# Gathering tokens for two experts at a time instead of four in a one-core decoder layer

## The chip, the cores and the metric

The kernel runs on one core of a Trainium2 chip. A core has TensorE (PE; its weight loads are listed as PEld), VectorE (DVE), ScalarE (ACT), GpSimd (POOL) and SyncE (SP, which here only issues DMAs), and 16 DMA engines. The metric is the device time of one execution in microseconds; the median of three executions of the kernel before is 1170.96 us (1170.91 to 1171.41).

## The reference

One layer of a decoder for 256 tokens of width 2048: a mixing part (pooling, sparse attention, cross attention, gates) that updates `x`, and then a mixture of 16 experts. Only the experts are touched here:

```python
lg = h @ w_router_group                      # 4 groups
g_top = argmax(lg)                           # every token goes to one group
le_sel = (h @ w_router_expert) of that group # 4 experts in it
pe_top, e_local = lax.top_k(softmax(le_sel), 2)
combine = one_hot(e_id) * weights            # two experts of one group per token
a = einsum('bsd,edf->bsef', h, w_e_gate)     # 16 x 2048 x 512
b = einsum('bsd,edf->bsef', h, w_e_up)
act = silu(a) * b * combine
x = x + einsum('bsef,efd->bsd', act, w_e_down)
```

All of it is in float32. Gate, up and down weights of the 16 experts are 192 MB.

## The kernel before, in words

The mixing part runs first (to about 720 us of the span), and loads of expert weights are mixed into its end. The experts follow in eight *pairs* of two experts (`pair`, L1101). A pair uses 24 weight tiles of 1 MB: 8 for gate, 8 for up, 8 for down (in the first pair gate and up alternate, table `FIRST`). Each weight tile of gate or up holds two k-tiles (128 rows of the 2048) for both experts, and takes 4 matmuls of 512 columns; each down tile takes 8 matmuls of 256 columns. The trace lists each of these float32 matmuls as two records.

*Gathering.* The tokens of four experts (a *quad*, one group) are picked at once by `Gather`. A 0/1 matrix `sel` (256 tokens by 4 x 64 places) is built on DVE from `slot`; the normalised input goes to 64 places per expert by matmuls: for each k-tile, `x2` is split into a high and a low part `xs` (ACT copies, DVE subtracts; three buffers, `split`), and four matmuls (high and low, two token halves) with `xs` as weights and `sel` as moving data give the gathered columns in PSUM. DVE multiplies them by the gain into `xg`, 16 k-tiles by 256 columns. One `step` does two k-tiles: 8 matmuls of 256 columns. The first quad is gathered between the gate and up tiles of pair 0; the later ones in pairs 1, 3 and 5: one step before and one behind the turning of the activations, and one behind each of six down tiles. Pairs 0, 2, 4 and 6 also compute the row factors of the quad (`factors`, four matmuls `sm<-cw,sel`) and turn `sel` for the way back (`back`, four transposes `sm<-ident,sel`, evacuated to `selT`).

*Scattering.* Behind each 512 columns of the down product, `scatter` splits them into high and low (`ob`), multiplies by `selT` (4 matmuls `sm<-ob,selT`) and adds the result into `x2`. A token belongs to one group, so the scattering of one quad never touches the tokens of the next; a quad's own tokens are gathered before its scattering.

*Order.* In this part each of PE, DVE, ACT and the loads on SP is pinned to the order in which the code is written. Weight tiles go round a ring of buffers (`order`: 4 `hq`, 9 `ex`, 8 of `raw` and `mx`: 21); one tile more, number 15 of the first pair, has its own buffer until pair 0 ends (`we15`). SP issues loads in the order of use, and each waits until PE has finished with the buffer's last tile. All PE work of the experts has line L840 (transposes L845), all DVE and ACT work L129.

Of the kernel before, what the change touches and what calls it, by code (L numbers as in the profile page):

```python
# [20 lines left out]
P = 128  # L21
NT = 2
# [33 lines left out]
def layer_kernel(tc, x, xT, memT, pos, cst, band, gains, bgate, wmem, wxq, widx, wkqvp, wpg, wgb, wo, wr, we, out):  # L56
# [5 lines left out]
    def pool(name, bufs=1, side=None, space=None, reuse="tile"):  # L62
        kw = {}
        if space is not None:
            kw["space"] = space
        else:
            kw["side"] = side or "left"
            kw["reuse_waits"] = reuse
        cm = tc.tile_pool(name=name, bufs=bufs, **kw)
        return cm, cm.__enter__()  # L70
# [67 lines left out]
    def sm_tile(shape, name="sm"):  # L138
        return sm.tile(shape, F32, tag="sm", name=name)
# [66 lines left out]
    def load(dst, src):  # L206
        tc.keep_in_program_order(nc.sync.dma_start(dst, src))
# [549 lines left out]
    def prefetch():  # L757
        pr, i = todo.popleft()
        kind = order.popleft()
        if kind == "raw":  # L760
            w = raw.tile([P, 4, 512], F32, tag="raw", name="wr")
        elif kind == "hq":
            w = htp.tile([P, 4, 512], F32, tag="hq", name="wh")
        elif kind == "ex":
            w = pools["exp"][1].tile([P, 4, 512], F32, tag="ew", name="we")
        else:
            w = mgp.tile([P, 4, 512], F32, tag=kind, name="wm", bufs=2)
        order.append(kind)
        if (pr, i) == (NE // 2 - 1, 23):
            load(w[:, 0:2], we[pr, i, :, 0:2])  # L770
            load(w[:, 2:4], we[pr, i, :, 2:4])
        else:
            load(w, we[pr, i])
        ahead.append(w)
# [63 lines left out]
    def pe(*a, **k):  # L838

        i = mm(*a, **k)  # L840
        tc.keep_in_program_order(i)
        return i

    def turn(ps, src):
        tc.keep_in_program_order(nc.tensor.transpose(ps, src, ident))  # L845
# [72 lines left out]

    c_w, wk = pool("work", side="right")

    pools["x"] = pool("early", side="right")
    et = pools["x"][1].tile([P, 4, 512], F32, name="we15")
    load(et, we[late])
    ahead.insert(use.index(late), et)

    def rt(shape, name):
# [11 lines left out]


    C = [P, NT * 5, 4, 4]  # L940
    xg0 = wk.tile([P, KD, 256], F32, tag="xg", name="xg")
    w = xg0[:, 14:16].rearrange("p a b -> p (a b)")
    Rc = w[:, 0:40].rearrange("p (t e) -> p t e", e=4)
    rank = w[:, 40:80].rearrange("p (t g e) -> p t g e", t=NT, e=4)
    ohg = w[:, 490:498].rearrange("p (t g) -> p t g", t=NT)
    c1 = w[:, 80:240].rearrange("p (t i j) -> p t i j", i=4, j=4)
    c2 = w[:, 240:400].rearrange("p (t i j) -> p t i j", i=4, j=4)
    E = w[:, 400:440].rearrange("p (t g e) -> p t g e", t=NT, e=4)
    EQ = 4
    SQ = EQ * 64  # L950

    def part(k, x0=None, dve=False):
# [36 lines left out]
    class Gather:  # L989
# [41 lines left out]

        def back(self, wp):

            self.selT = wp.tile([P, 2, S], F32R, tag="selT", name="selT")
            ps = sm_tile([P, 2, NT, P])
            for h in range(2):
                for t in range(NT):
                    turn(ps[:, h, t], self.flat[:, t, h * P : (h + 1) * P].bitcast(F32))
            A.activation(self.selT, ps.rearrange("p h t q -> p h (t q)"), AF.Copy)

        def factors(self):

            ps = sm_tile([P, 2, 2, 18])
            for h in range(2):
                for t in range(NT):
                    pe(ps[:, h], self.flat[:, t, h * P : (h + 1) * P], cw[:, t], start=t == 0, stop=t == NT - 1)
            self.f = wk.tile([P, 2, 2], F32, tag="fac", name="fac", bufs=2)
            fs = wk.tile([P, 2, 18], F32, tag="facs", name="facs")
            V.tensor_copy(fs, ps[:, :, 1])
            V.tensor_add(fs, fs, ps[:, :, 0])  # L1050
            for h in range(2):
                V.tensor_copy(self.f[:, h, 0:1], fs[:, h, NE : NE + 1])
                for e in range(2):
                    c = EQ * self.q + 2 * h + e
                    V.tensor_copy(self.f[64 * e : 64 * e + 64, h, 1:2], fs[64 * e : 64 * e + 64, h, c : c + 1])

    gf = cs[:, C_GFFN : C_GFFN + KD]
    ga = Gather(0, slot, parts0, xg0)
# [40 lines left out]
            next(open_.popleft(), None)  # L1099

    def pair(pr, slot_, store, ga):  # L1101
        hf = pr % 2

        def use_tile(ac, i):
            w = wtile()
            for kk in range(2):
                k = 2 * i + kk
                for e in range(2):
                    s0 = hf * P + 64 * e
                    pe(ac[64 * e : 64 * e + 64], ga.xg[:, k, s0 : s0 + 64], w[:, 2 * kk + e],  # L1110
                       start=k == 0, stop=k == KD - 1)

        def gathered(n):
            while 8 - len(ga.todo) < min(8, n):
                ga.step()

        nx = ga
        ag, au = acc_tile("gu"), None
        if pr == 0:
            au = acc_tile("gu")  # L1120
            for up, i in FIRST:
                gathered(i + 2)
                if (up, i) == (0, 7):
                    ga.factors()
                use_tile(au if up else ag, i)
                if (up, i) == (1, 0) and "x" in pools:
                    weights()
                    inorder.clear()
            if "x" in pools:
                close(pools.pop("x")[0])  # L1130
                pools["w2"] = pool("work2", side="right")
        else:
            for i in range(8):
                gathered(8)
                use_tile(ag, i)
                finish()
            if hf == 0:
                ga.factors()
            elif not store:
                nx = Gather(pr // 2 + 1, slot_, x0=ga.x0)  # L1140
                nx.split(3)
        w2 = pools["w2"][1]
        r2s, c1s = ga.f[:, hf, 0:1], ga.f[:, hf, 1:2]
        sg = w2.tile([P, FF], F32, tag="sg", name="sgm")
        A.activation(sg, ag, AF.Sigmoid, scale=r2s)
        V.scalar_tensor_tensor(sg, ag, r2s, sg, op0=ALU.mult, op1=ALU.mult)
        if au is None:
            au = acc_tile("gu")
            for i in range(8):
                use_tile(au, i)  # L1150
        for c in range(2):
            c = slice(c * FF // 2, (c + 1) * FF // 2)
            V.scalar_tensor_tensor(sg[:, c], sg[:, c], c1s, au[:, c], op0=ALU.mult, op1=ALU.mult)
        if hf == 0:
            ga.back(w2)
        elif nx is not ga:
            nx.step()
        aT = w2.tile([P, 4, P], F32, tag="aT", name="aT")
        for c in range(2):
            ps = sm_tile([P, 2, P])  # L1160
            for f in range(2):
                turn(ps[:, f], sg[:, (2 * c + f) * P : (2 * c + f + 1) * P])
            A.activation(aT[:, 2 * c : 2 * c + 2], ps, AF.Copy)
        if nx is not ga:
            nx.step()

        def scatter(ad, c0, n):
            ob = w2.tile([P, 2, 512], F32R, tag="ob", name="ob")[:, :, :n]
            A.activation(ob[:, 0], ad, AF.Copy)
            V.tensor_sub(ob[:, 1], ad, ob[:, 0])  # L1170
            yield
            for t in range(NT):
                ps = sm_tile([P, 512])[:, :n]
                for u in range(2):
                    pe(ps, ga.selT[:, hf, t * P : (t + 1) * P], ob[:, u], start=u == 0, stop=u == 1)


                ys = x2[:, t, c0 : c0 + n]
                V.tensor_add(ys, ys, ps)
                if store:  # L1180
                    nc.scalar.dma_start(out[t * P : (t + 1) * P, c0 : c0 + n], ys)

        def emit(ad, c0, n):

            g = scatter(ad, c0, n)
            next(g)
            open_.append(g)

        for n in range(4):
            ad = acc_tile("dn")  # L1190
            for i in range(2):
                if store and n == 3 and i == 1:
                    ad = acc_tile("dn")
                w = wtile()
                for k in range(4):
                    for e in range(2):
                        pe(ad[64 * e : 64 * e + 64, 256 * i : 256 * i + 256], aT[:, k, 64 * e : 64 * e + 64],
                           w[:, k, 256 * e : 256 * e + 256], start=k == 0, stop=k == 3)
                finish()
                if nx is not ga:  # L1200
                    nx.step()
                if store and n == 3:
                    emit(ad[:, 256 * i : 256 * i + 256], n * 512 + 256 * i, 256)
            if not (store and n == 3):
                emit(ad, n * 512, 512)
        if store:
            finish()
        return nx
# [34 lines left out]
            ga = pair(pr, slot, pr == NE // 2 - 1, ga)  # L1243

    close(pools["w2"][0])
    close(c_w)
    close(c_ht)
    close(c_ed)
# [86 lines left out]
```

## Time and profile before

| | |
|---|---|
| median of 3 runs | 1170.96 us |
| profiled execution | 1171.39 us, span 1169.4 us |
| PE busy | 1141.6 us, 98% |
| DVE busy | 579.1 us, 50% |
| ACT busy | 423.8 us, 36% |
| DMA | 342.44 MB, mean 293 GB/s |
| granted TensorE clock | 0.995 of full |

Busy time of PE is modelled, since matmuls are pipelined. So the distance from the start of one group of matmuls to the start of the next is the better measure of what it takes, and it is used below. A number in brackets behind a row of the timeline is idle time ahead of it, with what ended it.

### The profile page before, as it was taken

How to read it: one execution, taken by the hardware profiler on the slowest of the kernel's cores; microseconds unless marked ns; L12 is line 12 of the kernel's file. 1: busy time of each engine (PE TensorE's matmuls, PEld its weight loads, DVE VectorE, ACT ScalarE, POOL GpSimd, SP SyncE). 2: the span in 40 equal slices, each digit the busy share in tenths (PEclk: the TensorE clock that was granted, in tenths of full speed). 3: DMA queues.
4: the chain of work that ended last, by engine and by line, in shares of the span. 5: the costliest groups of instructions: out<-in, count | busy, mean ns of one | idle time of the engine just before them, and what ended most of it. 6: DMA issues, size and time to landing. Idle time of an engine off the chain costs nothing.

```text
span 1169.4 us, 14739 instructions
## 1 busy us (share of the span) xinstructions
PE 1141.6 (98%) x5847; PEld 786.6 (67%) x5847; DVE 579.1 (50%) x962; ACT 423.8 (36%) x672; POOL 28.9 (2%) x33
## 2 busy tenths in 40 slices
PE   8999999999999999999999999999999999999985
PEld 5788887888878888888888787454544645363423
DVE  7877468956636556556556445331412422250202
ACT  6665565445644444444444443211101201020000
POOL 3200000000000000000000000000000000000000
PEclk9999999999999999999999999999999999999998
DMA  9546554555545565565599859999999999999995
GB/s 384 188 149 225 180 180 153 180 180 174 208 174 203 192 212 199 191 208 203 190 340 363 316 192 351 423 423 426 426 427 426 427 426 427 427 425 427 426 428 216
DMA packets 50189, 342.44 MB, mean 293 GB/s; under 512 B 5696, under 2 KB 6336, under 8 KB 10432
## 3 DMA queue, kind: packets, MB, share of 16 engines
q1 hardware_dynamic: 46800, 331.93, 73.0%
q0 software_dynamic: 1728, 7.15, 1.7%
q10 hardware_dynamic: 1584, 2.34, 0.6%
q8 instruction: 48, 0.79, 0.2%
q14 instruction: 29, 0.24, 0.1%
HBM read 337.20 MB, written 4.19 MB: 292 GB/s over the span
## 4 chain that ended last, share of the span: by engine, by line


## 5 line engine op out<-in xcount | busy, mean ns | idle before, releaser
L282 PE MATMUL acc<-wh,hT 128*128 128x512 f32 (+1 forms) x1280 | 396.1, 388 | 0.0
L133 DVE TENSOR_TENSOR wl<-rawt,wh 128x1024 fp32r<-128x1024 f32 (+1 forms) x240 | 289.9, 1211 | 208.7 <-ACT wh L132 207.8
L132 ACT ACTIVATE wh<-rawt 128x1024 fp32r<-128x1024 f32 (+1 forms) x240 | 250.9, 1048 | 296.8 <-PE acc L282 289.9
L282 PEld LDWEIGHTS acc<-wh,hT 128*128 128x128 f32 x1280 | 238.3, 188 | 46.6 <-issue 0.3
L282 PE MATMUL acc<-wl,hT 128*128 128x512 f32 (+1 forms) x640 | 249.1, 389 | 0.0
L282 PEld LDWEIGHTS acc<-wl,hT 128*128 128x128 f32 x640 | 120.2, 188 | 23.9 <-DVE isc L593 0.3
L840 PE MATMUL gu<-we,xg 128*64 128x512 f32 x464 | 104.7, 596 | 4.6 <-DMA we<-in_we_dram 4.6
L282 PE MATMUL acc<-wh,mgT 128*128 128x512 f32 x256 | 80.3, 392 | 0.0
L840 PEld LDWEIGHTS gu<-we,xg 128*64 128x64 f32 x464 | 31.8, 137 | 68.9 <-issue 53.5
L129 DVE TENSOR_TENSOR x<-x,sm 128x512 f32<-128x512 f32 (+1 forms) x66 | 41.3, 668 | 32.6 <-PE sm L840 32.6
L129 ACT ACTIVATE ob<-dn 128x512 fp32r<-128x512 f32 (+1 forms) x33 | 19.2, 581 | 104.8 <-PE dn L840 98.2
L129 ACT ACTIVATE xs<-x 128x256 fp32r<-128x256 f32 x57 | 23.0, 415 | 90.0 <-PE sm L840 88.8
L282 PEld LDWEIGHTS acc<-wh,mgT 128*128 128x128 f32 x256 | 47.8, 188 | 10.0 <-issue 0.4
L129 DVE SCALAR_TENSOR_TENSOR sgm<-sgm,fac,gu 128x256 f32<-128x256 f32 x16 | 7.0, 478 | 92.0 <-PE gu L840 92.0
L282 PE MATMUL acc<-wl,mgT 128*128 128x512 f32 x128 | 50.5, 394 | 0.0
L129 DVE TENSOR_TENSOR ob<-dn,ob 128x512 fp32r<-128x512 f32 (+1 forms) x33 | 22.2, 673 | 55.9 <-ACT ob L129 55.9
L129 ACT ACTIVATE sgm<-gu,fac 128x512 f32<-128x512 f32 x8 | 5.5, 687 | 115.0 <-PE gu L840 68.0
L840 PE MATMUL gu<-wh,xg 128*64 128x512 f32 x200 | 45.1, 596 | 1.1 <-DMA wh<-in_we_dram 1.1
L840 PE MATMUL dn<-we,aT 128*64 128x256 f32 x384 | 45.6, 384 | 0.3
L840 PE MATMUL gu<-wm,xg 128*64 128x512 f32 x184 | 43.5, 593 | 0.5 <-DMA wm<-in_we_dram 0.5
L282 PE MATMUL acc<-wh,memT 128*128 128x512 f32 x128 | 41.8, 404 | 1.2 <-ACT wh L132 1.2
L840 PE MATMUL gu<-wr,xg 128*64 128x512 f32 x176 | 41.8, 595 | 0.5 <-DMA wr<-in_we_dram 0.5
(341 smaller groups left out, 1192.5 us busy)
## 6 DMA issues: line engine op xcount, KB each, us to landing
we<-in_we_dram SPq DMA_DIRECT2D x82, 1024.0 KB, 19.5
rawt<-in_wgb_dram SPq DMA_DIRECT2D x64, 1024.0 KB, 4.8
wh<-in_we_dram SPq DMA_DIRECT2D x37, 1024.0 KB, 19.6
wr<-in_we_dram SPq DMA_DIRECT2D x36, 1024.0 KB, 19.5
wm<-in_we_dram SPq DMA_DIRECT2D x36, 1024.0 KB, 19.5
rawt<-in_wkqvp_dram SPq DMA_DIRECT2D x24, 1024.0 KB, 4.8
rawt<-in_wo_dram SPq DMA_DIRECT2D x16, 1024.0 KB, 6.2
rawt<-in_wmem_dram SPq DMA_DIRECT2D x7, 1024.0 KB, 8.2
```

What stands on the lines that cost most here:

```text
L129: return lambda *a, **k: tc.keep_in_program_order(getattr(self.e, name)(*a, **k))
L132: pin(A.activation(hi, ps, AF.Copy))
L133: pin(V.tensor_sub(lo, ps, hi))
L282: m = mm(o, a[:, c], w[:, kk], start=st, stop=sp)
L840: i = mm(*a, **k)
```

## The change

`EQ`, the number of experts in one gather, goes from 4 to 2. `Gather` is made for each pair instead of each second pair; `sel` has 128 columns, `selT` half its rows, `xg` is 16 k-tiles by 128 columns, 8 KB per partition instead of 16 KB. The freed 8 KB hold one weight tile more, kind `e2`, which joins the ring (22 buffers) and is first loaded right behind `we15`.

Since two pairs now share a group's tokens, the next pair's tokens have to be gathered before the present pair's scattering changes them. `follow` turns `sel`, makes the next `Gather` and splits three parts; it stands ahead of the up tiles (in pair 0 behind gate and up). One step runs behind each of up tiles 1 to 7, writing the k-tiles of the same `xg` that the up matmuls have finished with, and the eighth behind the turning of the activations. In pair 0 all eight run among the first three down tiles. `finish`, which runs the waiting scatter, comes behind the steps instead of ahead of them.

```diff
+        elif kind == "e2":
+            w = pools["e2"][1].tile([P, 4, 512], F32, tag="e2", name="wn")
...
+    pools["e2"] = pool("more", side="right")
+    order.appendleft("e2")
...
     load(et, we[late])
+    prefetch()
...
-    xg0 = wk.tile([P, KD, 256], F32, tag="xg", name="xg")
+    xg0 = wk.tile([P, KD, P], F32, tag="xg", name="xg")
-    EQ = 4
+    EQ = 2
...
+        def follow():
+
+            ga.back(w2)
+            if store:
+                return ga
+            g = Gather(pr + 1, slot_, xg=ga.xg, x0=ga.x0)
+            g.split(3)
+            return g
...
             au = acc_tile("gu")
+            nx = follow()
             for i in range(8):
                 use_tile(au, i)
+
+                if i > 0 and nx is not ga:
+                    nx.step()
...
-        if hf == 0:
-            ga.back(w2)
-        elif nx is not ga:
-            nx.step()
+        if pr == 0:
+            nx = follow()
...
+                if nx is not ga:
+                    for _ in range(8 if n else 2 if pr == 0 else 1):
+                        nx.step()
                 finish()
-                if nx is not ga:
-                    nx.step()
```

On PE, pair 1 from its last up tiles on, in the kernel before (`sm<-sel,xs` x8 is one step of a gather, `gu` gate or up, `dn` down, `sm<-ident,sgm` the turning of the activations, `sm<-ob,selT` a scatter):

```order
L840 MATMUL gu<-wm,xg 64x512 x4
L840 MATMUL gu<-wr,xg 64x512 x4
L840 MATMUL sm<-sel,xs 128x256 x8
L845 MATMUL sm<-ident,sgm 128x128 x4
L840 MATMUL sm<-sel,xs 128x256 x8
L840 MATMUL dn<-wm,aT 64x256 x8
L840 MATMUL sm<-sel,xs 128x256 x8
L840 MATMUL dn<-wr,aT 64x256 x8
```

The same place in the changed kernel, from the end of the gate tiles on:

```order
L842 MATMUL sm<-cw,sel 128x36 x2
L847 MATMUL sm<-ident,sel 128x128 x2
L842 MATMUL gu<-we,xg 64x512 x8
L842 MATMUL sm<-sel,xs 128x128 x8
L842 MATMUL gu<-we,xg 64x512 x4
...
L842 MATMUL gu<-wm,xg 64x512 x4
L842 MATMUL sm<-sel,xs 128x128 x8
L847 MATMUL sm<-ident,sgm 128x128 x4
L842 MATMUL sm<-sel,xs 128x128 x8
L842 MATMUL dn<-wr,aT 64x256 x8
```

A step still has 8 matmuls, with 128 columns in place of 256. Every pair but the last now holds eight of them, where before only pairs 0, 1, 3 and 5 did.

On PE in pair 0, from the turning of the activations on, in the changed kernel (before, no step stands there):

```order
L847 MATMUL sm<-ident,sgm 128x128 x4
L842 MATMUL sm<-sel,xs 128x128 x8
L842 MATMUL dn<-wr,aT 64x256 x8
L842 MATMUL sm<-sel,xs 128x128 x16
L842 MATMUL dn<-wm,aT 64x256 x8
L842 MATMUL sm<-sel,xs 128x128 x16
L842 MATMUL dn<-wr,aT 64x256 x8
L842 MATMUL sm<-sel,xs 128x128 x24
L842 MATMUL sm<-ob,selT 128x512 x4
```

Four of the eight steps follow another step directly there, and the first scatter comes behind all of them.

On DVE in pair 1, from the multiplication by the gate on, in the changed kernel (`xg<-sm,cs` ends a step, `sgm<-sgm,fac,gu` is the product that the turning waits for):

```order
L129 SCALAR_TENSOR_TENSOR sgm<-gu,fac,sgm 128x512
L129 TENSOR_TENSOR sel<-cs,slot 128x128 x2
L129 TENSOR_TENSOR xs<-x_4893,xs 128x256 x4
L129 TENSOR_TENSOR xg<-sm,cs 128x256
...
L129 TENSOR_TENSOR xs<-x_4893,xs 128x256 x2
L129 TENSOR_TENSOR xg<-sm,cs 128x256
L129 SCALAR_TENSOR_TENSOR sgm<-sgm,fac,gu 128x256 x2
L129 TENSOR_TENSOR xg<-sm,cs 128x256
```

The product now stands behind the multiplication that ends the seventh step; before, it stood ahead of the first.

## Rows read from the trace of the kernel before

**Rows 1.** The page's 40 slices of the span: PE busy and DMA, in tenths.

```profile
PE   8999999999999999999999999999999999999985
...
DMA  9546554555545565565599859999999999999995
```

**Rows 2.** Busy time by windows, pairs 0 to 7: PE, PEld, DVE, ACT, POOL, clock, DMA share, GB/s.

```profile
725.64:781.36 55.72, 55.60 (x331) 26.89 (x330) 21.79 (x67) 9.70 (x22) 0.00 (x0) 1.00 1.01 420
781.36:837.54 56.18, 56.18 (x342) 28.97 (x342) 21.51 (x46) 9.66 (x23) 0.00 (x0) 1.00 1.01 426
837.54:886.47 48.93, 48.80 (x287) 21.89 (x284) 10.63 (x23) 4.29 (x8) 0.00 (x0) 1.00 1.01 427
886.47:942.61 56.14, 56.14 (x342) 28.92 (x340) 20.81 (x41) 9.69 (x23) 0.00 (x0) 1.00 1.01 426
942.61:991.53 48.92, 48.78 (x286) 21.88 (x284) 10.63 (x23) 4.29 (x8) 0.00 (x0) 1.00 1.01 427
991.53:1047.67 56.14, 56.14 (x342) 28.93 (x340) 20.81 (x41) 9.68 (x23) 0.00 (x0) 1.00 1.01 426
1047.67:1096.60 48.93, 48.80 (x286) 21.89 (x284) 10.63 (x23) 4.29 (x8) 0.00 (x0) 1.00 1.01 426
1096.60:1156.03 59.43, 51.09 (x278) 19.95 (x274) 9.59 (x16) 4.23 (x8) 0.00 (x0) 1.00 0.97 405
```

**Rows 3.** Timeline of PE in pair 7: start, us, engine, line, tiles, count, idle before.

```profile
1099.55 3.65 PE L840 MATMUL gu<-wh,xg 128*64 128x512 f32 x16
1103.78 1.94 PE L840 MATMUL gu<-wh,xg 128*64 128x512 f32 x8 [0.58 <-DMA wh<-in_we_dram]
...
1133.08 1.94 PE L840 MATMUL gu<-wm,xg 128*64 128x512 f32 x8 [0.52 <-DMA wm<-in_we_dram]
```

**Rows 4.** Timeline of PE, end of pair 2's up tiles and the turning.

```profile
863.57 1.89 PE L840 MATMUL gu<-wr,xg 128*64 128x512 f32 x8
865.29 1.89 PE L840 MATMUL gu<-wm,xg 128*64 128x512 f32 x8
867.11 0.66 PE L845 MATMUL sm<-ident,sel 128*128 128x128 f32 x4
867.76 0.83 PE L845 MATMUL sm<-ident,sgm 128*128 128x128 f32 x4
```

**Rows 5.** Timeline of PE, the first steps of quad 0 between gate and up tiles.

```profile
722.34 1.14 PE L309 MATMUL warm<-ident 128*128 128x128 f32 x8
723.32 2.33 PE L840 MATMUL sm<-sel,xs 128*128 128x256 f32 x16
725.64 3.65 PE L840 MATMUL gu<-wh,xg 128*64 128x512 f32 x16
729.23 1.22 PE L840 MATMUL sm<-sel,xs 128*128 128x256 f32 x8
730.38 3.65 PE L840 MATMUL gu<-wh,xg 128*64 128x512 f32 x16
```

**Rows 6.** Timeline of PE, the narrow matmuls of the factors in pair 4.

```profile
957.74 0.62 PE L840 MATMUL sm<-cw,sel 128*128 128x36 f32 x4
958.29 1.94 PE L840 MATMUL gu<-wr,xg 128*64 128x512 f32 x8
```

**Rows 7.** Groups by line and form from 690 us on: busy, mean ns, idle before.

```profile
L129 DVE TENSOR_TENSOR xs<-x,xs 128x256 fp32r<-128x256 f32 x57 | 23.5, 421 | 27.3 <-ACT xs L129 26.7
...
L129 ACT ACTIVATE xs<-x 128x256 fp32r<-128x256 f32 x57 | 23.0, 415 | 90.0 <-PE sm L840 88.8
...
L129 DVE TENSOR_TENSOR x<-x,sm 128x256 f32<-128x256 f32 x4 | 1.5, 418 | 1.0 <-PE sm L840 1.0
```

**Rows 8.** Busy time by windows of 2 us about the first extra load.

```profile
720.00:722.00 2.00, 1.88 (x17) 1.68 (x16) 1.83 (x9) 1.64 (x4) 0.00 (x0) 1.00 0.95 295
722.00:724.00 2.00, 1.74 (x16) 1.76 (x17) 1.15 (x5) 0.00 (x0) 0.00 (x0) 1.00 0.92 369
...
730.00:732.00 2.00, 2.00 (x12) 0.87 (x12) 1.25 (x9) 1.36 (x3) 0.00 (x0) 1.00 0.84 332
```

More of the change, by code (lines that the diff above doesn't have):

```diff
@@ L940, in layer_kernel @@
     C = [P, NT * 5, 4, 4]
-    xg0 = wk.tile([P, KD, 256], F32, tag="xg", name="xg")
-    w = xg0[:, 14:16].rearrange("p a b -> p (a b)")
+    xg0 = wk.tile([P, KD, P], F32, tag="xg", name="xg")
+    w = xg0[:, 12:16].rearrange("p a b -> p (a b)")
     Rc = w[:, 0:40].rearrange("p (t e) -> p t e", e=4)
@@ L1032, in back @@
         def back(self, wp):
[L1034 to L1039, printed above, removed]
-        def factors(self):
[L1043 to L1055, printed above, removed]
+            self.selT = wp.tile([P, S], F32R, tag="selT", name="selT")
+            ps = sm_tile([P, NT, P])
+            for t in range(NT):
+                turn(ps[:, t], self.flat[:, t].bitcast(F32))
+            A.activation(self.selT, ps.rearrange("p t q -> p (t q)"), AF.Copy)
+        def factors(self):
+            ps = sm_tile([P, 2, 18])
+            for t in range(NT):
+                pe(ps, self.flat[:, t], cw[:, t], start=t == 0, stop=t == NT - 1)
+            self.f = wk.tile([P, 2], F32, tag="fac", name="fac", bufs=2)
+            fs = wk.tile([P, 50], F32, tag="facs", name="facs")[:, :18]
+            V.tensor_copy(fs, ps[:, 1])
+            V.tensor_add(fs, fs, ps[:, 0])
+            V.tensor_copy(self.f[:, 0:1], fs[:, NE : NE + 1])
+            for e in range(2):
+                c = EQ * self.q + e
+                V.tensor_copy(self.f[64 * e : 64 * e + 64, 1:2], fs[64 * e : 64 * e + 64, c : c + 1])
     gf = cs[:, C_GFFN : C_GFFN + KD]
@@ L1101, in pair @@
     def pair(pr, slot_, store, ga):
-        hf = pr % 2
         def use_tile(ac, i):
@@ L1108, in use_tile @@
                 for e in range(2):
-                    s0 = hf * P + 64 * e
+                    s0 = 64 * e
                     pe(ac[64 * e : 64 * e + 64], ga.xg[:, k, s0 : s0 + 64], w[:, 2 * kk + e],
@@ L1136, in pair @@
                 finish()
-            if hf == 0:
[L1138 to L1141, printed above, removed]
-        w2 = pools["w2"][1]
-        r2s, c1s = ga.f[:, hf, 0:1], ga.f[:, hf, 1:2]
+            ga.factors()
+        w2 = pools["w2"][1]
+        r2s, c1s = ga.f[:, 0:1], ga.f[:, 1:2]
+        def follow():
[5 more added lines that the diff above has]
+            return g
         sg = w2.tile([P, FF], F32, tag="sg", name="sgm")
@@ L1153, in pair @@
             V.scalar_tensor_tensor(sg[:, c], sg[:, c], c1s, au[:, c], op0=ALU.mult, op1=ALU.mult)
-        if hf == 0:
-            ga.back(w2)
-        elif nx is not ga:
-            nx.step()
+        if pr == 0:
+            nx = follow()
         aT = w2.tile([P, 4, P], F32, tag="aT", name="aT")
@@ L1174, in scatter @@
                 for u in range(2):
-                    pe(ps, ga.selT[:, hf, t * P : (t + 1) * P], ob[:, u], start=u == 0, stop=u == 1)
+                    pe(ps, ga.selT[:, t * P : (t + 1) * P], ob[:, u], start=u == 0, stop=u == 1)
                 ys = x2[:, t, c0 : c0 + n]
@@ L1245, in layer_kernel @@
     close(pools["w2"][0])
+    close(pools["e2"][0])
     close(c_w)
```

## The prediction

> **What bounds the kernel now.** I read the 40 slices of the page first. PE is at nine tenths nearly throughout, and from about slice 25 on, where the experts are computed, the DMA is too [rows 1]. Two resources look full, and only one of them can set the pace at a time, so the second view is a table of windows cut at the pairs [rows 2]. The DMA moves 420 to 427 GB/s in pairs 0 to 6, whatever the pair holds. But the pairs do not last equally long: those with a gather of the next quad take 56.18, 56.14 and 56.14 us, those without 48.93, 48.92 and 48.93. Every pair uses 24 tiles, so a DMA that set the pace would make them equal. It is PE that does.
>
> What a pair would take at the DMA's pace is read in the third view, the timeline of the last pair. From 1103.78 on, each tile's first matmul waits for its load [rows 3]; from there to 1133.08 are 12 tiles, 29.30 us, or 2.44 us a tile and 58.6 us for 24. So PE begins with a stock of loaded tiles, eats them faster than they come (48.9 or 56.1 us against 58.6), and runs out of them only in pair 7. There it waits. Pair 7 has no factors and no turned `sel` of its own, so PE's work in it is that of pair 6 less 0.55 us for the four factor matmuls [rows 6] and 0.65 us for the four transposes [rows 4]: 48.93 - 0.55 - 0.65 = 47.73. It lasts 59.43 [rows 2]. PE therefore has 59.43 - 47.73 = 11.7 us to spare in the whole expert part, all at its end. More work for PE is free up to 11.7 us; beyond that it lengthens the kernel one for one. That is the question to put to this change.
>
> **The change part by part.**
>
> *The steps of the gather.* Before, 4 gathers of 8 steps, 32; now 8 gathers, 64, each with the same 8 matmuls, whose moving data is half as wide. What a matmul of 128 columns costs here (with its own weights of 128 x 128 each time) is the unknown. From start to next start, steps of 256 columns take 2.32 us for 16 and 1.15 for 8, so 0.144 us each; full float32 matmuls of 128 columns take 0.98 us for 8, 0.123 each [rows 5]; the factor matmuls, with the same kind of data and only 36 columns, take 0.55 for 4, 0.138 each [rows 6]. A seventh of the columns saves next to nothing, so something other than columns sets the spacing, and 128 columns should lie between these. I take 0.13: a step costs 1.04 us instead of 1.15. The ends are 0.072 (half of 0.144, if columns alone counted) and 0.144 (no saving).
>
> Between gate or up tiles a step costs more than itself. Two tiles and a step take 730.38 - 725.64 = 4.74 us [rows 5], two tiles alone 2 x 1.72 [rows 4], so the step costs 1.30; with the narrower matmuls 1.30 - 0.11 = 1.19.
>
> The Trainium skill (TensorE: Matmul & The Clock Gate, LDWEIGHTS) gives a load of stationary weights a time that goes with its columns, 107 ns for 128 at its formula, whatever the moving side does. The 36-column row agrees with such a floor. The same page (Back-to-back issue gap) states about 81 ns for a sustained matmul of 128 columns; no row here is as short, and what it would make of the time is a rival below.
>
> *Pairs 1 to 6.* I start from a pair without a gather, 48.93. The factors now take two matmuls, half of 0.55: -0.28. The transposes of `sel` halve: -0.33 of 0.65. Seven steps behind up tiles: 7 x 1.19 = 8.33. The eighth, behind the turning, where ACT's copies of the turned activations run beside it: 1.04. The turning itself waits for DVE's product, which is now queued behind the multiplication that ends the seventh step; that costs one DVE operation of 128x256 from PSUM, 0.42 [rows 7], and its handover, 0.5 with an estimate of 0.1 for the latter. Sum: 58.2 us. Six of these are 349.1; before, the six windows sum to 315.24. The difference is +33.9.
>
> The splitting doubles as well: 16 parts a pair at 0.415 on ACT and 0.421 on DVE, and eight multiplications at about 0.42 [rows 7]. A step needs 2 x 0.421 + 0.42 = 1.26 us of DVE and arrives every 1.72 + 1.19 = 2.91 us, so it is hidden behind PE. A pair without a gather has DVE busy 10.63 us and ACT 4.29 [rows 2]; 10 and 7 us more leave both far from full. In the up stage `xg` is overwritten in place, but a block behind the matmuls that read it, so no wait.
>
> *Pair 0.* Its six steps among the tiles save 6 x 0.11, the halved factors and transposes 0.61. Added are eight steps among three down tiles, 8 x 1.04 = 8.3. Four of them follow a step directly, and there DVE's 1.26 rules over PE's 1.04: 0.9 more. The first of them also waits for DVE to build `sel` and two parts behind the product: some 1.2, an estimate from two parts at 0.42 and as much again for `sel`, ACT working alongside. Sum: 55.72 - 0.66 - 0.61 + 8.3 + 0.9 + 1.2 = 64.9, or +9.1. The two steps ahead of pair 0 save 16 x 0.014 = 0.2.
>
> *The tile more in the ring.* It is loaded behind `we15`, near 720 us. A tile more ahead of time is worth 2.44 us if the DMA would stand idle, and if the DMA sets the end. In the windows there, the DMA is busy 0.95, 0.92 and 0.84 of 2 us, with the others about full [rows 8]: 0.1 + 0.16 + 0.32, some 0.6 us to fill, and nothing before, since the buffer comes free only then. With PE as the bound throughout, it is worth nothing. I take 0, and 0.6 at best.
>
> *The sum.* PE: -0.2 + 9.1 + 33.9 = +42.8 us. Of this, 11.7 go into the waits of pair 7, which vanish: its tiles arrive by the DMA's own clock about as before, and PE comes to it 42.8 us later. Left: +31.1. What follows the last down tile is unchanged. Against the profiled execution, 1171.39 + 31.1 = 1202.5; the median of the runs is 0.43 lower: 1202 us.
>
> **The rivals.**
>
> *A: columns count, and the DMA keeps the end (not slower).* If a matmul of 128 columns took half of 0.144, a step would be 0.58 and one between up tiles 1.30 - 0.57 = 0.73. A pair would be 48.93 - 0.61 + 7 x 0.73 + 0.58 = 54.0, six of them +8.8; pair 0 would change by -0.61 - 6 x 0.57 + 8 x 0.58 = +0.6, the two first steps by -1.1. With the waits at the turning and in pair 0 gone too, which shorter steps could bring, PE's +8.3 would vanish in the 11.7, the last pair would wait for loads as now, and the tile more would fill up to 0.6 us: 1170.4 to 1171. It decides from the point where PE is given less than 11.7 us of work. For it: 128 columns at the rate of 256. Against it: the 36-column row. Within this, the time could fall by up to 2.44 us if more DMA idle time were found than the windows show, to 1168.5.
>
> *B: narrow matmuls follow each other closer than the rows for them.* At 0.10 us, halfway between the half and my value, 0.03 less each, a step is cheaper by 0.24. Six pairs lose 6 x 8 x 0.24 = 11.5 of their 33.9, pair 0 loses 14 x 0.24 = 3.4 of 9.1, the two first steps 0.5: 42.8 - 15.4 = +27.4 for PE, 15.7 beyond the spare 11.7: 1187. For it: the rows of narrow matmuls are few and short, with a change of operation at each end. Against it: 8 matmuls of 128 columns in a row at 0.123.
>
> The 81 ns of the Trainium skill (TensorE: Matmul & The Clock Gate, Back-to-back issue gap) lie on this side; an estimate worked out from them in the same way is 1177 us.
>
> *C: no saving at all and more waits.* Steps at 1.30, the eighth at 1.15, 1 us of waiting at each turning: 48.93 - 0.61 + 9.1 + 1.15 + 1 = 59.6 a pair, +42.2; pair 0 +12: 1171 + 42.5 = 1213. Narrow matmuls give ACT and DVE less time for the parts, with three buffers between them; the distance of 2.91 us between steps speaks against it.
>
> **How the numbers follow.** What a measurement of this kernel can tell from no change is about 0.2%, 2.3 us. My forecast has 0.74 with its own range 1188 to 1209. B has 0.11, C 0.06. A has 0.06 with the time about unchanged, and 0.03 with a gain of over 2.3 us. Slower: 0.74 + 0.11 + 0.06 = 0.91; same 0.06; faster 0.03. The range is 1180 to 1213: it takes in B and C with some room below B, and leaves out A.
>
> **What would show it.** In the profile after, the pairs 1 to 6 should all last about the same, 58 us, each with some 64 matmuls `sm<-sel,xs` of 128 columns, 1.0 to 1.1 us for eight. Pair 7 should last about 47.7 with no matmul waiting for a load. Pair 0 should last about 65, with PE waiting for `xs` between the consecutive steps. DMA should stay near 420 GB/s until some 30 us before the end, and then fall to little: the last tiles lie ready. I am wrong if eight such matmuls take under 0.7 us, or if the last pair's tiles still wait for their loads.

## The result, and the profile after

The changed kernel takes 1209.79 us (median of 4 runs, 1208.8 to 1209.84), the kernel before 1171.01 us (4 runs, 1170.91 to 1171.41). The ratio is 1.0327, with a 95% interval of 1.0314 to 1.0341: slower by 38.8 us. The profiled execution of the changed kernel took 1209.84 us, its span 1208.1. The forecast was 1202 us, with a range of 1180 to 1213. Of all executions reported below one was slowed throughout (1227.29 us, with 64 columns a matmul), and it is left out of that kernel's time and ratio.

The slices first, as in [rows 1]: the DMA over the span after.

```profile
DMA  9546554545655555565889589899999999999932
```

The DMA is now finished early. Its last two slices are at three and two tenths, where [rows 1] have nine and five. The table of windows, cut at the pairs after, with the columns of [rows 2]:

```profile
724.75:791.35 66.60, 64.63 (x392) 34.70 (x391) 28.33 (x90) 15.69 (x38) 0.00 (x0) 0.97 0.93 376
791.35:851.51 60.16, 58.83 (x347) 29.33 (x347) 20.00 (x51) 10.42 (x24) 0.00 (x0) 0.97 0.99 407
851.51:909.97 58.46, 57.13 (x347) 28.58 (x345) 19.29 (x46) 10.45 (x24) 0.00 (x0) 1.00 1.01 426
909.97:968.46 58.49, 57.16 (x347) 28.57 (x345) 19.30 (x46) 10.45 (x24) 0.00 (x0) 1.00 1.01 426
968.46:1028.63 60.17, 58.84 (x347) 29.34 (x345) 19.30 (x46) 10.45 (x24) 0.00 (x0) 0.97 1.01 426
1028.63:1087.09 58.46, 57.13 (x347) 28.57 (x345) 19.29 (x46) 10.45 (x24) 0.00 (x0) 1.00 1.01 426
1087.09:1145.58 58.49, 57.16 (x347) 28.58 (x345) 19.30 (x46) 10.45 (x24) 0.00 (x0) 1.00 1.01 426
1145.58:1194.84 49.26, 48.57 (x282) 21.26 (x279) 10.30 (x21) 4.50 (x9) 0.00 (x0) 1.00 0.36 146
```

Three things are to be seen beside [rows 2]. Pairs 1 to 6 are alike now, and sum to 354.23 us against 315.24, +39.0. Pair 0 grew by 10.9. Pair 7 shrank by 10.2, and the DMA moves only 146 GB/s in it: the loads no longer hold anything up. With a start 0.9 us earlier this makes 39.0 + 10.9 - 10.2 - 0.9 = +38.8. (The start of pair 0 is no effect of the change that could be told: in the profiled executions of two variants below that differ from the changed kernel only behind it, product_first and the one with both edits, it lies at 724.28 and 725.77.) The second thing is the clock column. In pairs 1 and 4, and in pair 0, it is 0.97, and pairs 1 and 4 last 1.7 us longer than their like. The third is that PE is busy 1.33 us less than each window of pairs 1 to 6, where [rows 2] have it full or within 0.14 us.

Where this idle time lies, the timeline of PE shows, here the end of the up tiles of pair 6 (columns as in [rows 3]):

```profile
1120.92 1.11 PE L842 MATMUL sm<-sel,xs 128*128 128x128 f32 x8
1121.96 1.94 PE L842 MATMUL gu<-we,xg 128*64 128x512 f32 x8
1123.83 1.11 PE L842 MATMUL sm<-sel,xs 128*128 128x128 f32 x8
1126.27 0.80 PE L847 MATMUL sm<-ident,sgm 128*128 128x128 f32 x4 [1.33 <-DVE sgm L129]
1126.82 1.09 PE L842 MATMUL sm<-sel,xs 128*128 128x128 f32 x8
1127.84 5.40 PE L842 MATMUL dn<-we,aT 128*64 128x256 f32 x48
1133.17 1.20 PE L842 MATMUL sm<-ob,selT 128*128 128x512 f32 x4
```

A step takes 1121.96 - 1120.92 = 1.04 us, 0.130 a matmul. A tile behind a step takes 1.87 from its start to the next, where one behind a tile takes 1.72 [rows 4], so a step among tiles costs 1.04 + 0.15 = 1.19. Behind the seventh step PE stands 1.33 us until DVE's product `sgm` is there. DVE's own rows at that time say why:

```profile
1124.97 0.42 DVE L129 TENSOR_TENSOR xs<-x,xs 128x256 fp32r<-128x256 f32 x1 [1.81 <-ACT xs L129]
1125.32 0.42 DVE L129 TENSOR_TENSOR xg<-sm,cs 128x256 f32<-128x256 f32 x1
1125.65 0.86 DVE L129 SCALAR_TENSOR_TENSOR sgm<-sgm,fac,gu 128x256 f32<-128x256 f32 x2
```

And ACT's row of the same part:

```profile
1124.52 0.42 ACT L129 ACTIVATE xs<-x 128x256 fp32r<-128x256 f32 x1 [2.04 <-PE sm L842]
```

The last up tile's matmuls stand ahead of the step that began at 1123.83, so the product could have run about then (product_first below shows that it can). But DVE is pinned to the order of the code, and two operations stand ahead of it. The first is a part for the eighth step. It waits for ACT's half of that part, which ACT starts only at 1124.52, when PE gives it a buffer. Only then come the multiplication that ends the step, and the product.

The clock is seen in windows of 1 us, first behind the same wait in pair 1, then in pair 2 (columns as in [rows 2]; the clock is the third value from the end):

```profile
830.00:831.00 1.00, 0.42 (x3) 0.26 (x4) 0.83 (x3) 0.00 (x0) 0.00 (x0) 1.00 1.01 426
831.00:832.00 1.00, 1.00 (x10) 1.00 (x10) 0.00 (x0) 0.77 (x2) 0.00 (x0) 0.95 1.03 434
832.00:833.00 1.00, 1.00 (x7) 0.69 (x7) 0.42 (x1) 0.00 (x0) 0.00 (x0) 0.50 1.01 426
...
835.00:836.00 1.00, 1.00 (x12) 0.60 (x10) 0.00 (x0) 0.00 (x0) 0.00 (x0) 0.84 1.04 442
...
893.00:894.00 1.00, 1.00 (x12) 0.69 (x10) 0.00 (x0) 0.00 (x0) 0.00 (x0) 1.00 0.99 418
```

In pair 1 the granted clock falls to 0.50, the level of 1.2 GHz, from 832 to past 835, and the down tiles of that time take longer; in pair 2 it stays at 1.00. Both had PE idle for the same 1.33 us.

Pair 0 has a wait of another origin. PE's timeline there:

```profile
762.24 0.80 PE L847 MATMUL sm<-ident,sgm 128*128 128x128 f32 x4 [1.81 <-DVE sgm L129]
762.83 1.90 PE L842 MATMUL sm<-sel,xs 128*128 128x128 f32 x8
764.66 3.11 PE L842 MATMUL dn<-wr,aT 128*64 128x256 f32 x16
767.70 2.18 PE L842 MATMUL sm<-sel,xs 128*128 128x128 f32 x16
769.81 1.95 PE L842 MATMUL dn<-wm,aT 128*64 128x256 f32 x16
```

And ACT's timeline of the same kernel, the row of the sigmoid:

```profile
760.10 0.69 ACT L129 ACTIVATE sgm<-gu,fac 128x512 f32<-128x512 f32 x1 [12.16 <-PE gu L842]
```

The sigmoid needs the gate tiles alone, but starts only when the last tile of the stage is done, and with it the product is late. PE waits 1.81 us, and the clock falls once more (the first down tile takes 3.04 us to the next row's start; in pair 6 the three of the row at 1127.84 take 5.33, 1.78 each). The two consecutive steps at 767.70 take 2.11 us to the next row's start, 1.05 each.

### The profile page after: what moved, and what is told of

The parts are those of the page before. It is cut to its first block, busy times and chain, and to the rows that moved or that the text cites. A ratio compares the mean times of both kernels' runs of the same rounds, so it can differ in the third digit from the quotient of the medians.

```text
span 1208.1 us, 15496 instructions
## 1 busy us (share of the span) xinstructions
PE 1179.5 (98%) x6103; PEld 816.2 (68%) x6103; DVE 607.0 (50%) x1074; ACT 450.7 (37%) x740; POOL 30.2 (3%) x33
## 4 chain that ended last, share of the span: by engine, by line
## 5 line engine op out<-in xcount | busy, mean ns | idle before, releaser
L129 DVE TENSOR_TENSOR xs<-x,xs 128x256 fp32r<-128x256 f32 x121 | 49.5, 421 | 92.3 <-ACT xs L129 92.3
L842 PE MATMUL gu<-we,xg 128*64 128x512 f32 x416 | 93.8, 596 | 0.0
L842 PEld LDWEIGHTS sm<-sel,xs 128*128 128x128 f32 x512 | 62.6, 193 | 41.0 <-issue 40.1
L129 ACT ACTIVATE xs<-x 128x256 fp32r<-128x256 f32 x121 | 48.7, 416 | 107.5 <-PE sm L842 105.7
L842 PE MATMUL sm<-sel,xs 128*128 128x128 f32 x512 | 71.5, 283 | 0.2
L842 PEld LDWEIGHTS gu<-we,xg 128*64 128x64 f32 x416 | 28.5, 137 | 51.8 <-issue 47.8
L842 PE MATMUL dn<-we,aT 128*64 128x256 f32 x480 | 55.5, 383 | 0.1
L842 PE MATMUL gu<-wr,xg 128*64 128x512 f32 x208 | 49.9, 600 | 0.0
L842 PE MATMUL gu<-wm,xg 128*64 128x512 f32 x208 | 49.7, 598 | 0.0
```

What stands on the lines that cost most here:

```text
L129: return lambda *a, **k: tc.keep_in_program_order(getattr(self.e, name)(*a, **k))
```

## Experiments

Each ratio is to runs of the kernel before on the same chip; the changed kernel stands at 1.0327.

**The extra tile.** The changed kernel without it:

```diff
-    order.appendleft("e2")
...
-    prefetch()
```

> The changed kernel (1209.8 us) without the extra weight tile in the ring. My theory, that TensorE's own work sets the end: the tile is worth nothing, 1209.8 us within 1. Rival, that loads still count: one tile less ahead of time costs its 2.44 us, 1212.2.

Measured: 1209.61 us, ratio 1.0326 (1.0309 to 1.0343). The tile is worth nothing here, since PE sets the end. In the profiled execution the clock fell in pairs 1 and 5 this time, beside pair 0.

**Half the matmuls of the gather:**

```diff
-                    for h in range(2):
-                        pe(ps[:, kk], xs[:, h, t], self.flat[:, t], start=t + h == 0, stop=t + h == 2)
+                    pe(ps[:, kk], xs[:, 0, t], self.flat[:, t], start=t == 0, stop=t == 1)
```

> The changed kernel with the low parts left out of the gather: 4 matmuls a step instead of 8, all splitting, multiplying and waiting kept. Theory (number of gather matmuls, 0.130 us each): 64 steps lose 4 x 0.130 = 0.52, 33.3 us, so 1176.5; down to the loads' bound of about 1171 at the least. Rival (what DVE and ACT do around the steps costs the time): under 12 us less, above 1198.

Measured: 1183.25 us, ratio 1.0096 (1.0079 to 1.0112): 26.5 us below the changed kernel. The window of pair 3 in it, in which the clock did not fall:

```profile
899.12:954.26 55.14, 53.58 (x315) 25.00 (x313) 19.29 (x46) 9.78 (x24) 0.00 (x0) 1.00 1.01 426
```

And PE's timeline of pair 1, the last two steps ahead of the turning with the tile between them:

```profile
817.20 0.66 PE L842 MATMUL sm<-sel,xs 128*128 128x128 f32 x4
817.79 1.94 PE L842 MATMUL gu<-wm,xg 128*64 128x512 f32 x8
819.66 0.66 PE L842 MATMUL sm<-sel,xs 128*128 128x128 f32 x4
821.88 0.92 PE L847 MATMUL sm<-ident,sgm 128*128 128x128 f32 x4 [1.55 <-DVE sgm L129]
```

So the matmuls are most of the loss: 256 were left out, as many as the change adds. Of the 6.8 us that are missing from the 33.3 expected, some 4.5 lie in the step itself. It takes 817.79 - 817.20 = 0.59 us for four matmuls, not 0.52 as half of 1.04, and there are 64 steps. Four matmuls more thus cost 1.04 - 0.59 = 0.45, 0.11 each, and the rest of a step, about 0.14, does not go with their number. The remainder went into waits and the clock: the wait at the turning grew to 1.55, because DVE's work is the same and PE arrives earlier, and in the profiled execution the clock fell in four pairs (0, 1, 2 and 6) instead of three.

**Columns.** Each step's matmuls on 256 columns (the same 128 read twice, as wide as in the kernel before), and on 64:

```diff
-                        pe(ps[:, kk], xs[:, h, t], self.flat[:, t], start=...
+                        pe(ps[:, kk], xs[:, h, t], self.flat[:, t].unsqueeze(1).to_broadcast([P, 2, SQ]), start=...
```
```diff
-                        pe(ps[:, kk], xs[:, h, t], self.flat[:, t], start=...
+                        pe(ps[:, kk, :64], xs[:, h, t], self.flat[:, t, :64], start=...
```

> The changed kernel with each gather matmul streaming its 128 columns twice (256 columns, the second half not used). Theory (the spacing does not go with columns): 0.144 instead of 0.130 us, 512 matmuls, 7 us more, 1217. Rival (columns set the cost): the spacing doubles, 512 x 0.130 = 66 us more at the full proportion and 27 us at one column a cycle of 2.4 GHz (128 / 2.4 = 53 ns), 1237 to 1276.

> The changed kernel with 64 columns a gather matmul instead of 128 (the second expert of a pair is given the first one's tokens). Theory (the spacing does not go with columns): 1209.8, at most 2 us less. Rival (columns count): 512 matmuls lose half of 53 ns at the least, 13.6 us, 1196 or less.

Measured: 1213.47 us (1.0357, 1.034 to 1.0375) and 1204.82 us (the median of three, 1204.8 to 1208.62; 1.0299, 1.0274 to 1.0324). A step and the next tile, in PE's timeline of pair 2, with 256 columns:

```profile
873.50 1.21 PE L842 MATMUL sm<-sel,xs 128*128 128x256 f32 x8
874.65 1.94 PE L842 MATMUL gu<-wm,xg 128*64 128x512 f32 x8
```

The same two rows with 64 columns:

```profile
872.27 1.08 PE L842 MATMUL sm<-sel,xs 128*128 128x64 f32 x8
873.28 1.94 PE L842 MATMUL gu<-wm,xg 128*64 128x512 f32 x8
```

Start to start that is 1.15 for 256 columns and 1.01 for 64, with 1.04 for 128 between them. A quarter of the columns saves an eighth of the time, and no rival in which columns set the price holds. The single matmuls in the traces show where the columns are felt (medians over the 42 steps among up tiles): the first two matmuls of a step start 0.133, 0.164 and 0.222 us apart with 64, 128 and 256 columns, all later ones 0.112, 0.112 and 0.120. Both totals are below what was expected of them by the steps alone: in neither profiled execution did the clock fall in pairs 1 to 6, which gives back some 3.4 us.

**DVE's order alone.** The seventh step's operations of DVE go behind the product; PE's order stays:

```diff
-                if i > 0 and nx is not ga:
+                if 0 < i < 7 and nx is not ga:
                     nx.step()
...
         if pr == 0:
             nx = follow()
+        elif nx is not ga:
+            nx.step()
```

> The changed kernel with the seventh step issued behind DVE's product instead of ahead of it, in pairs 1 to 6; TensorE's order stays the same, only DVE takes the product before the multiplication of the seventh step. Theory (1.33 us of idle TensorE ahead of each turning is a wait for the product behind that multiplication): six waits fall from 1.33 to about 0.1, 7.4 us less; if the drops of the granted clock in pairs 1 and 4 (1.7 us each) follow from these waits, they vanish too: 1199. Without that: 1202.4. Rival (the turning waits for something else): 1209.8.

Measured: 1195.84 us, ratio 1.0207 (1.0187 to 1.0227), 14 us below the changed kernel. PE's timeline at the turning of pair 1:

```profile
827.68 1.11 PE L842 MATMUL sm<-sel,xs 128*128 128x128 f32 x8
828.63 0.62 PE L847 MATMUL sm<-ident,sgm 128*128 128x128 f32 x4
```

DVE's timeline there, the row of the product:

```profile
827.80 0.87 DVE L129 SCALAR_TENSOR_TENSOR sgm<-sgm,fac,gu 128x256 f32<-128x256 f32 x2 [0.79 <-PE gu L842]
```

And the window of pair 2:

```profile
847.74:904.51 56.77, 56.77 (x346) 28.53 (x344) 19.37 (x46) 10.34 (x24) 0.00 (x0) 1.00 1.01 426
```

The product now runs beside the seventh step, PE does not wait, and the pair is 1.7 us shorter. Six times that is 10 us; the clock, which stays at 1.00 in pairs 1 to 6 of this profiled execution, gives 3.4 more. No matmul was taken out.

**Buffers in pair 0.** The changed kernel halves `selT`, and that shifts the buffers behind it. Here it has its old size, half of it unused; then the same with DVE's order as above:

```diff
-            self.selT = wp.tile([P, S], F32R, tag="selT", name="selT")
+            self.selT = wp.tile([P, 2, S], F32R, tag="selT", name="selT")[:, 0]
```

> The changed kernel with selT given its old size again (its second half unused), nothing else. In pair 0 of the changed kernel ACT's first sigmoid starts at 760.10, when the up tiles have ended, though its gate tiles ended at about 756.4; before, it ran at 758.44 beside the last up tiles. Theory: the smaller selT moves the buffer of the sigmoid onto that of the tile we15, which the last up tile still reads; with the old size the wait of 1.81 us ahead of the turning falls to about 0.3, and if the drop of the clock behind it (1.3 us) follows from the wait, that goes too: 1207. Rival (the order of the instructions causes it): 1209.8.

> product_first and selT_padded together. Theory: the gains add, 1195.8 less 1.5 to 3, 1193 to 1194.5. Still above the kernel before, since the 64 steps remain. Rival: as product_first, 1195.8.

Measured: 1207.55 us (1.0311, 1.0294 to 1.0328) and 1194.28 us (1.0198, 1.0181 to 1.0215). With `selT` padded alone, ACT's timeline has the sigmoid of pair 0 at:

```profile
756.93 0.69 ACT L129 ACTIVATE sgm<-gu,fac 128x512 f32<-128x512 f32 x1 [8.73 <-PE gu L842]
```

PE's timeline there has the turning:

```profile
760.90 0.89 PE L847 MATMUL sm<-ident,sgm 128*128 128x128 f32 x4 [0.22 <-DVE sgm L129]
```

And the windows of its pairs 0 and 1:

```profile
725.01:788.49 63.48, 63.06 (x391) 33.72 (x390) 28.16 (x90) 15.58 (x38) 0.00 (x0) 1.00 0.97 391
788.49:850.21 61.72, 60.39 (x347) 30.53 (x346) 20.00 (x51) 10.43 (x24) 0.00 (x0) 0.94 0.98 404
```

The sigmoid starts 3.17 us earlier, ahead of the last tiles, and pair 0 is 3.1 us shorter. So the sigmoid's output had come to lie where a tile was still being read. That it was a buffer is shown by the padding; which tile, the trace doesn't say (the code opens the pool of `sgm` where that of `we15` is closed, so `we15` is likely). Part of the gain is lost in pair 1, whose clock fell for longer here, 0.94. With both edits no pair is below 1.00, and the kernel is still 2% above the one before.

**What the spare of pair 7 buys.** In the kernel before, the matmuls of its second gather are issued twice; then those of all gathers, 256 more:

```diff
             for kk in range(2):
...
+                if self.q == 1:
+                    for t in range(NT):
+                        for h in range(2):
+                            pe(ps[:, kk], xs[:, h, t], self.flat[:, t], start=...
```

(`if True:` in the second.)

> The kernel before, with the 8 matmuls of each step of quad 1 issued twice: 64 more matmuls of 256 columns, 7.7 to 9.2 us more work for TensorE in pair 1. Theory (11.7 us to spare, all in the waits of pair 7): no change, 1171 within 0.6, and pair 7 shorter by what pair 1 is longer. Rival (TensorE, 98% busy, has nothing to spare): 1179 to 1180.

> The kernel before, with the 8 matmuls of every step issued twice: as many more matmuls (256) as the change adds, but in the old places, with no doubled splitting and the old buffers. Theory: 256 x 0.12 to 0.144 = 31 to 37 us more for TensorE, less the spare 11.7: 1190 to 1196. Rival (all of it counts): 1202 to 1208. Rival (the change costs by its waits and doubled splitting, not by the matmuls): under 1180.

Measured: 1174.93 us, ratio 1.0019 (1.001 to 1.0029), and 1189.52 us, ratio 1.0151 (1.0134 to 1.0169). For the first, the windows of pairs 1 and 7:

```profile
781.93:845.79 63.86, 63.86 (x406) 36.62 (x406) 22.14 (x46) 9.72 (x23) 0.00 (x0) 1.00 0.99 414
1104.85:1160.73 55.88, 50.15 (x278) 20.29 (x274) 9.58 (x16) 4.23 (x8) 0.00 (x0) 1.00 0.97 404
```

And two of its windows of 4 us, at the end of pair 1 and behind it:

```profile
840.00:844.00 4.00, 4.00 (x30) 2.61 (x28) 1.63 (x3) 0.00 (x0) 0.00 (x0) 1.00 0.86 311
844.00:848.00 4.00, 4.00 (x27) 1.99 (x27) 1.64 (x3) 0.60 (x1) 0.00 (x0) 1.00 0.88 299
```

I expected no change, and it is 0.2% slower. Pair 1 grew by 7.7 us, but pair 7 gave back only 3.6: a slower PE early on frees the buffers later, the DMA runs out of free ones (311 and 299 GB/s, where the kernel before has 422 and 428), and what it loses there it lacks at the end. The five windows of 4 us from 836 to 856, at 412, 311, 299, 313 and 373 GB/s, lack what takes 4.0 us at 426. So the 11.7 us are not a store for any work at any place; in this profiled execution they fell short by some 4 us for work in pair 1. In the second kernel the window of pair 7 shrank by 11.2 us:

```profile
1125.99:1174.19 48.20, 47.53 (x279) 20.89 (x275) 9.59 (x16) 4.22 (x8) 0.00 (x0) 1.00 0.80 332
```

There the spare was used nearly whole, and the extra matmuls beyond it went into the time, +17.7 us. Together that is some 29 us of PE for 256 matmuls, near the 26.5 of half_gather. With the change, pairs 0 to 6 last 39.0 + 10.9 = 49.9 us longer, so that some 21 us of it are not the price of 256 matmuls more.

**A tile less in the kernel before:** `NEX = 8` for 9.

> The kernel before with a ring of 20 weight tiles instead of 21 (eight of kind ex instead of nine). Theory: in the kernel before the loads pace the last pair, and a tile that was loaded before 700 us, when the DMA had idle time, now comes behind them: 2.44 us more, 1173 to 1174. Rival (the size of the ring does not matter): 1171 to 1171.8.

Measured: 1173.52 us, ratio 1.0019 (1.001 to 1.0029), 2.3 us more (1.2 to 3.4 by the interval). Where loads pace the end that agrees with one tile's 2.44 us. The ring matters in the kernel before, and no longer in the changed one.

## Why the prediction was right, point by point

The time lies in the stated range, but 0.8 us above the 1188 to 1209 that I gave my own account; the range reached further because it made room for rival C. The forecast was nearly 8 us too low. By the windows, pairs 1 to 6 were 5.1 too low and pair 0 1.7, the gain in pair 7 was 1.5 too high, and the start came 0.7 earlier than I had it.

**The bound.** That PE sets the pace, and the loads only the end of pair 7, held: the loads' waits vanished, DMA kept 426 GB/s through pairs 2 to 6 and had little left in pair 7. The gain in pair 7 was 10.2, not 11.7. I left out that pair 7 now has its own factors and transposes of `sel` (0.61 us for the two). And I counted its wait for the product (0.58, the same before and after) among the waits for loads, which vanish; it stays. Both are to be seen here in PE's timeline after:

```profile
1160.68 0.40 PE L842 MATMUL sm<-cw,sel 128*128 128x36 f32 x2
1160.93 0.44 PE L847 MATMUL sm<-ident,sel 128*128 128x128 f32 x2
...
1175.83 0.83 PE L847 MATMUL sm<-ident,sgm 128*128 128x128 f32 x4 [0.58 <-DVE sgm L129]
```

**The step.** 0.13 a matmul, 1.04 a step and 1.19 among tiles came out exactly. The 0.13 is a step's average: inside a step the matmuls are 0.112 apart, and the rest lies at its ends. Rival A fell with it: columns hardly count. Rival B's 0.10 was not seen either, nor the 81 ns which the Trainium skill (TensorE: Matmul & The Clock Gate, Back-to-back issue gap) states for 128 columns: even inside a step of 64 columns it was 0.112, and 1.01 / 8 = 0.126 on average. What the Trainium skill gives in the LDWEIGHTS section of that page, a load whose time goes with the weights' columns (107 ns for 128), fits better with a price that the moving side hardly changes; 0.112 lies 5% above it.

**Pairs 1 to 6.** Forecast +33.9, measured +39.0. The term that failed is the wait at the turning: "one DVE operation of 128x256 from PSUM, 0.42 [rows 7], and its handover, 0.5". It was 1.33 of idle PE, since a part for the next step, and ACT's half of it, stood ahead of the product too; that the product was late by DVE's order is shown by product_first. An undisturbed pair still came to 58.47 us on average of four, 0.27 above the forecast. That it came so near is luck: the wait's excess of 0.8 was set against some 0.6 that I had too much, above all for the eighth step. That fills time in which PE waited for ACT's copies of the turned activations before, as PE's timeline of the kernel before shows in pair 6, where no gather runs:

```profile
1077.89 0.83 PE L845 MATMUL sm<-ident,sgm 128*128 128x128 f32 x4
1078.86 1.95 PE L840 MATMUL dn<-we,aT 128*64 128x256 f32 x16
```

From the turning to the first down tile are 0.97 us there, in which the weight load of the down tile waits 0.37 for ACT, and 1127.84 - 1126.27 = 1.57 after, so the step added 0.60 instead of 1.04. Six times 0.27 is 1.6. The other 3.4 us are the clock, at half in pairs 1 and 4 for some 3 us each, of which the prediction knew nothing.

**Pair 0.** Forecast 64.9, measured 66.60, but not in my way. The 0.9 us for DVE's pace between consecutive steps did not come: 16 matmuls take 2.11 us. I had added up DVE's operations at 0.42 us each, 1.26 a step; but in DVE's rows above one starts 0.33 to 0.35 us behind the other (1124.97, 1125.32, 1125.65), so three need about 1.0. What came was the late sigmoid with the fall of the clock behind it, together 3.1 us, as selT_padded shows; without them the pair takes 63.48, 1.4 below the forecast. That 66.60 lies near 64.9 is luck.

**The tile more.** 0, as forecast, and shown by no_extra_tile.

**The sum.** With DVE's order and the buffer mended, 1194.28 us, some 15.5 of the 38.8 are gone. That is the price of the waits with what the clock did behind them. The remaining 23 are the gather's doubled steps, as the windows of the kernel with both edits show. Its pairs 1 to 6 last 56.77 to 56.85 us, PE busy throughout. That is 0.7 more than pairs 1, 3 and 5 took with the wide gather [rows 2], and 0.6 of it are factors and transposes that they now have of their own: a gather of half the width costs no less than the wide one did. Pairs 2, 4 and 6, which had none, take 7.8 to 7.9 more each. Pairs 1 to 6 make +25.5 together, pair 0 +7.8, and pair 7, at 48.95, gives back 10.5. Rival C's total, 1213, was nearest in time, and the waits at the turning that it asked for (1 us) did come; its steps without any saving are refuted by the 1.04.

## What to carry to other kernels

Halving the moving side of short matmuls that each bring their own weights saved little here; if their number doubles, count them at nearly the full price. When work is put in front of a handover, walk through the queue of the engine that hands over: everything queued there ahead of the result, with what that waits for in turn, is the length of the wait, and moving the result up in that queue took no instruction more here and gave back 14 us. A wait at the end of a kernel is spare time in full only for work that doesn't slow the loads that feed it (of 7.7 us in pair 1, 3.6 came back), or once there is so much work that the loads no longer set the end (11.2 of 11.7).

## What was not expected of the hardware

Gaps of 1.33 us in PE's work were followed by the half clock in two of six pairs, at a cost of about 1.7 us each, more than the gap itself. Which pairs it hit differed from one profiled execution to the next (1 and 4 in the changed kernel, 1 and 5 without the extra tile, 1, 2 and 6 in half_gather), with the same wait in all six; with the wait gone (product_first, and both edits), it hit none of the six. The Trainium skill (TensorE: Matmul & The Clock Gate, Part 1) describes a monitor of PE's activity that runs on its own time, not the program's; that agrees with pairs of one kind being treated differently. That the gaps cause the falls is argued from this and not shown. Whether a shorter gap would be safe, the runs don't tell: with 256 columns and with 64 the clock never fell in pairs 1 to 6 though PE waited there too (1.31 and 1.20 us in pair 2), and why is open.
